# Gate projections first and block products for eight of the conv mixer's projections, in one Trainium2 kernel of a hybrid decoder trunk

## The chip, the cores and the metric

One Trainium2 chip, and one of its cores: the kernel uses no other. The metric is the device time of one execution in microseconds (us), lower is better. The kernel before was run three times: 1012.56, 1013.74 and 1014.99 us, median 1013.74.

## The reference

The reference is a trunk of two layers on 512 tokens of 1024 features, all in float32. The change touches only the first layer's mixer, a short gated convolution:

```
def short_conv_mixer(h, w_in, conv_w, w_out):
    bcx = h @ w_in
    b_gate, c_gate, u = jnp.split(bcx, 3, axis=-1)
    y = b_gate * causal_depthwise_conv3(c_gate * u, conv_w)
    return y @ w_out
...
mix = short_conv_mixer(rmsnorm(h, a_pre_norm[l]), a_w_in[l], a_conv_w[l], a_w_out[l])
h = h + rmsnorm(mix, a_post_norm[l])
```

The three taps run along the tokens. After the mixer come a SwiGLU block (FFN) of layer 0, a layer of sliding-window attention, and the FFN of layer 1; all norms are RMS norms with a gain.

## The kernel before, in words

**Numbers.** Every float32 product is made of three matmuls on rounded halves: each operand is split into a high part (a rounding copy on ACT) and a low part (a subtraction on DVE). `mm3` writes the three matmuls, lines 205 to 207. So each weight tile of 128 x 1024 costs one ACT copy (L490, whi) and one DVE subtraction (L491, wlo) before PE can use it.

**The conv mixer.** The 1024 features are eight tiles of 128, numbered f = 0 to 7. For each tile there are three projections, c, u and b, each a job of 24 matmuls of 128x512 on one weight tile (`conv_jobs`, `project`). PE works on the raw x times the norm gain; the row of reciprocal norms, one number for each token, is multiplied in when DVE takes a job's result from its PSUM bank: `first` takes c (L767), `second` takes u (L770), after which GpSimd (POOL) multiplies the two (L771), `taps` are one TENSOR_SCALAR and two SCALAR_TENSOR_TENSOR on DVE (L774, L777), `third` takes b on DVE (L783) and multiplies on POOL (L784, giving y). For f = 7 the multiplications are on DVE.

**The output projection.** The first four y go in pairs through seven block products P1 to P7 (`seven`, Strassen's scheme, with sums of the blocks of y made by `pair_sums`, L602 to L612); their results are collected in the mix tiles, first by ACT copies (L658), then by DVE adds or subtractions (L660). The last four y are split (`yhi` L788 on ACT, `ylo` L789 on DVE) and used with the weight tiles w0 to w3 in the closing products, whose matmuls write the banks named pmix. The fourth contraction step of the closing's first token tile needs y of f = 7.

**The order.** The opening stage (token halves, tiles f = 0 and 1, norm row) is written out by hand. Then the string `CONV` lists the jobs, and `in_line` runs it: it writes the matmuls of job j, then prepares the weights of job j + 3 (`LINE_LEAD`), then takes steps from the list `late`, into which the jobs put their DVE, ACT and POOL steps. All of this is inside a manual schedule, so each engine executes its instructions in the written order and waits at the first that is not ready. Weights arrive through a queue of SyncE (SP) into seven tiles (`N_RAW`); four split weights (`N_W`) can be held at once. POOL also issues the DMAs that add up blocks of later weights in DRAM (`hsum`, L559), started by `sum_on` at named jobs.

**PSUM.** Eight banks: four in `ps_mm`, two in `ps_sc`, two in `ps_pt`. A bank is handed out in turn within its pool, and the new user waits for the last reader of the old one. P1, P6, P7, P4 collect in two `ps_mm` banks (px), P5 and P3 in the two `ps_sc` banks (pz), P2 in the two `ps_pt` banks (py). The job b6 has its bank in `ps_sc` as well (the string "mms" for f = 6 in the list of pools).

Of the kernel before, what the change touches and what calls it, by code (L numbers as in the profile page):

```python
# [13 lines left out]
ALU = mybir.AluOpType  # L14
# [23 lines left out]
    "c2 u2 b2 c3 u3 b3 c4 u4 b4 c5 u5 P1 P5 b5 P6 P3 c6 P7 P2 u6 P4 b6 w0 c7 u7 w1 b7 w2 w3"  # L38
)

# [41 lines left out]
def yoco_kernel(  # L82
# [8 lines left out]
    w_in: bass.AP,  # L91
    w_ob: bass.AP,
# [134 lines left out]
    xt = [halves("xt") for _ in range(KT // 2)]  # L227
    xt = [xt[k // 2][k % 2] for k in range(KT)]
# [217 lines left out]
    class Raw:  # L446


        def __init__(self, *srcs):
            self.srcs = srcs  # L450
            self.widths = [s.shape[0] * S if len(s.shape) == 3 else D for s in srcs]
            self.n = sum(self.widths)

        def fetch(self):
            self.tile, c = wraw.tile([P, D], F32, tag="raw", name=name("raw")), 0
            for src, n in zip(self.srcs, self.widths):
                dst = self.tile[:, c : c + n]
                if len(src.shape) == 3:
                    src, dst = (src.rearrange("k p c -> p k c"),
                                dst.rearrange("p (k c) -> p k c", c=S))  # L460
                nc.sync.dma_start(dst, src)
                c += n

    class Job:
# [10 lines left out]
        def add(self):  # L475
            if self.make:
                raw = self.raws[0].tile
                nc.vector.tensor_tensor(out=raw, in0=raw, in1=self.raws[1].tile, op=ALU.add)  # L478
# [16 lines left out]
    def in_line(jobs, late, paced=True):  # L495
# [9 lines left out]
        def prepare(j):  # L505

            if 0 <= j < len(jobs):
                jobs[j].prepare()
            while n[0] < len(raws) and (n[0] < N_RAW or raws[n[0] - N_RAW].last <= j):
                raws[n[0]].fetch()  # L510
                n[0] += 1
            if j + 1 < len(jobs):
                jobs[j + 1].add()
# [4 lines left out]
        for j, job in enumerate(jobs):  # L518
# [5 lines left out]
            for _ in range(1 if paced else max(len(late) - 1, 1)):  # L524
                if late and not job.alone:
                    late.pop(0)()
# [141 lines left out]
    rows = slot("rrow")  # L668
# [6 lines left out]
    sums = small.tile([P, 4], F32, tag="sums", name=name("sums"))  # L675
    squares = wide("squares")

    def square(b):
        nc.scalar.activation(squares, hs[b], AF.Square, scale=1 / 32,
                             accum_out=sums[:, b : b + 1])  # L680

    with tc.manual_schedule(engines=ALL):

        warm = small.tile([P, 1], F32, tag="warm", name=name("warm"))
        nc.scalar.activation(warm, ones[:, 0:1], AF.Copy)
        idle = bank("idle", ps_pt)
        for _ in range(WARM):
            nc.tensor.matmul(idle[:, :P], ones, ones, start=True, stop=True)

        def first_hi(i, c0, c1):  # L690
            nc.scalar.activation(ws[i][0][:, c0:c1], first[i][:, c0:c1], AF.Copy)

        def first_lo(i, c0, c1):
            nc.vector.tensor_tensor(out=ws[i][1][:, c0:c1], in0=first[i][:, c0:c1],
                                    in1=ws[i][0][:, c0:c1].bitcast(F32), op=ALU.subtract)

        def token_hi(k):
            nc.scalar.activation(xs[k][0], xt[k], AF.Copy, scale=g(G_APRE, k))

        def token_lo(k):  # L700
            nc.vector.scalar_tensor_tensor(
                out=xs[k][1], in0=xt[k], scalar=g(G_APRE, k), in1=xs[k][0].bitcast(F32),
                op0=ALU.mult, op1=ALU.subtract,
            )

        FIRST = {0: [(0, 0, P), (0, P, 384)], 1: [(0, 384, 768)], 2: [(0, 768, D), (1, 0, S)],
                 4: [(1, S, D)], 5: [(2, 0, S)], 6: [(2, S, D)]}
        for k in range(KT):
            pieces = FIRST.get(k, [])
            token_hi(k)  # L710
            for p in pieces:
                first_hi(*p)
            for p in pieces:
                first_lo(*p)
            token_lo(k)
            for i in range(3):
                for t in range(3):
                    n = 3 * k + t
                    whi, wlo = (w[:, n % KT * P : (n % KT + 1) * P] for w in ws[n // KT])
                    nc.tensor.matmul(begun[0][t], (whi, wlo, whi)[i], xs[k][i == 2],  # L720
                                     start=k == i == 0, stop=k == KT - 1 and i == 2)
        later += [fetch(w_in[1, t]) for t in range(len(later), 3)]
        for b in range(NB):
            hs[b] = wide("h")
            nc.sync.dma_start(hs[b], x[b])
        nc.sync.dma_start(mask, tables[:, 2 * S :])
        nc.sync.dma_start(snk, sinks.partition_broadcast(P))
        ws = [split_weights(None, raw, True) for raw in later[:2]]
        square(0)
        square(1)  # L730
        ws.append(split_weights(None, later[2], True))
        square(2)
        square(3)
        project(begun[1][0], ws[0], xs)
        v = small.tile([P, 4], F32, tag="v", name=name("v"))
        nc.vector.tensor_scalar(out=v, in0=sums, scalar1=EPS, scalar2=None, op0=ALU.add)
        nc.gpsimd.tensor_tensor(out=cols, in0=v, in1=mhalf, op=ALU.pow)
        project(begun[1][1], ws[1], xs)
        pr = bank("pr", ps_pt)
        dg, dhi, dlo = slot("dg"), slot("dhi", F32R), slot("dlo", F32R)  # L740
        for b in range(NB):
            nc.vector.tensor_scalar(out=dg[:, b * P : (b + 1) * P], in0=ident,
                                    scalar1=cols[:, b : b + 1], scalar2=None, op0=ALU.mult)
        nc.scalar.activation(dhi, dg, AF.Copy)
        nc.vector.tensor_tensor(out=dlo, in0=dg, in1=dhi.bitcast(F32), op=ALU.subtract)
        nc.tensor.matmul(pr, ones_r, dlo, start=True, stop=False)
        nc.tensor.matmul(pr, ones_r, dhi, start=False, stop=True)
        nc.scalar.activation(rows, pr, AF.Copy)
        nc.vector.tensor_scalar(out=nsnk, in0=snk, scalar1=-1.0, scalar2=None, op0=ALU.mult)
# [5 lines left out]
    def conv(f, pc=None, pu=None, pb=None):  # L755

        eng = nc.gpsimd if f < KT - 1 else nc.vector
        cr, ur = halves("cru")
        cu, t = halves("cut")
        br, y = halves("bry")  # L760
# [11 lines left out]

        def taps():
# [8 lines left out]
        def third(pb):  # L782
            nc.vector.tensor_tensor(out=br, in0=pb, in1=rows, op=ALU.mult)  # L783
            eng.tensor_tensor(out=y, in0=t, in1=br, op=ALU.mult)  # L784
# [14 lines left out]

        return first, second, taps, third, end  # L800

    def conv_jobs(f, pools):
# [10 lines left out]
        def then(i):  # L813
            def steps():
                first, second, taps, third, end = steps_of
                if i < 2:
# [3 lines left out]
                    if f == KT - 1:  # L820
                        taps()
                        return []
                    return [taps]
# [12 lines left out]
    with tc.manual_schedule(engines=ALL):  # L836
        project(begun[1][2], ws[2], xs)

        def late():
            parts = []  # L840
            for f in range(2):
                first, second, taps, third, end = conv(f)
                first(begun[f][0])
                second(begun[f][1])
                parts += [taps, lambda third=third, f=f: third(begun[f][2])]
                sum_on(f"c{f}")
                issue(len(issues))
            return parts + end()


        product = seven(acts, 2, mix_c, True)
        b11, b12, b22, b21 = (Raw(w_ob[b]) for b in range(4))
        line = {
            f"P{p}": Job(raws, lambda job, p=p: product(p, range(2), *job.w), None, len(raws) > 1)
            for p, *raws in ((1, b11), (5, b11, b12), (6, b11, b22), (3, b22), (7, b12, b22),
                             (2, b21), (4, b11, b21))
        }
        pools = {"p": ps_pt, "m": ps_mm, "s": ps_sc}
        for f, of in zip(range(2, KT), ("ppm", "mmm", "ssp", "mmp", "mms", "spm")):
            for c, job in zip("cub", conv_jobs(f, [pools[p] for p in of])):  # L860
                line[f"{c}{f}"] = job
        for n in range(4):
            line[f"w{n}"] = closing = Job([Raw(w_out[n // 2, n % 2])], None)
            closing.slots = True
        in_line([line[n] for n in CONV.split()], late, False)
        ws = [line[f"w{n}"].w for n in range(4)]
# [787 lines left out]
def _lay_out(x, a_pre_norm, a_w_in, a_conv_w, a_w_out, a_post_norm, ffn_pre_norm,  # L1654
# [39 lines left out]
    for b in (0, HD):  # L1694
# [9 lines left out]
    wi = c(wi[[1, 2, 0]].transpose(1, 0, 2, 3))  # L1704
    wi[0] = wi[0].reshape(3, P, KT, P).transpose(2, 0, 1, 3).reshape(3, KT, P, P).transpose(
# [13 lines left out]
        "w_in": wi,  # L1719
        "w_ob": c(blocks(np.asarray(a_w_out[0])[: D // 2])),  # L1720
# [26 lines left out]
```

## Time and profile before

| what | value |
|---|---|
| median of 3 runs | 1013.74 us (1012.56 to 1014.99) |
| the profiled execution | 1012.5 us, of which the span of the profile is 1010.7 us |
| POOL busy | 203.9 us, 20% |
| ACT busy | 588.4 us, 58% |
| jobs of the conv line end, first pmix matmul | 155.37 us |

A row of the profile's timeline is: start, duration, engine, line, operation, output<-input, shapes, and in brackets the idle time of that engine ahead of the row and what ended it. A row of its stretches is: from:to, PE busy, busy time of each engine with the number of instructions, the granted clock as a share, the share of the DMA engines, GB/s. In the groups by line, busy time and mean duration come first and idle time ahead of the group's instructions after the second bar.

### The profile page before, as it was taken

What the parts mean: (1) busy time and instruction counts of PE and PEld (TensorE: products, weight loads), DVE (VectorE), ACT (ScalarE), POOL (GpSimd) and SP (SyncE); (2) the same over time, 40 slices, a digit from 0 to 9 for tenths busy, and PEclk for the clock granted to TensorE, in tenths of its full rate; (3) what the DMA queues carried; (4) which work ended last, traced back from release to release, by engine and by line L of the source; (5) the groups of instructions that cost most, each with busy time, mean ns of one, the idle gap of its engine ahead of it and who ended that gap; (6) DMA issues with size and microseconds to landing.
All of it is one profiled execution on the core that took longest, in us unless ns stands there. A gap on an engine that the chain in (4) does not pass through costs nothing.

```text
span 1010.7 us, 16083 instructions
## 1 busy us (share of the span) xinstructions
PE 1002.3 (99%) x5864; PEld 882.4 (87%) x5864; DVE 887.7 (88%) x1525; ACT 588.4 (58%) x1061; POOL 203.9 (20%) x264
## 2 busy tenths in 40 slices
PE   9999999999999999999999999999999999999997
PEld 8888888999889898898898888789998888989986
DVE  5766767899789999999888998888997999999996
ACT  6322444875656465566385788777666564645641
POOL 0443033102101011000022657321211010110001
PEclk9999999999999999999999999999999999999999
DMA  9997789649979789779603889966999577979742
GB/s 357 293 252 241 180 248 334 185 167 268 334 246 288 250 287 311 240 214 343 209 1 120 225 236 245 303 233 176 295 288 330 167 247 235 284 277 266 247 174 84
DMA packets 66575, 244.50 MB, mean 242 GB/s; under 512 B 7872, under 2 KB 8384, under 8 KB 54720
## 3 DMA queue, kind: packets, MB, share of 16 engines
q1 hardware_dynamic: 51328, 145.98, 38.8%
q0 software_dynamic: 14592, 96.48, 37.6%
q10 hardware_dynamic: 576, 1.02, 0.3%
q8 instruction: 46, 0.75, 0.3%
q14 instruction: 33, 0.27, 0.1%
HBM read 237.15 MB, written 102.76 MB: 336 GB/s over the span
## 4 chain that ended last, share of the span: by engine, by line
PE 97%; DVE 2%; ACT 1%; issue 0%; DVEq 0%
PE gx L1093 15%; PE gx L1096 8%; PE pcub L207 4%; PE pcub L205 4%; PE pcub L206 4%; PE px L206 4%; PE px L205 4%; PE px L207 4%; PE pmix L207 3%; PE pmix L205 3%; PE pmix L206 3%; PE gz L1093 3%; PE gy L206 2%; PE gy L205 2%; PE gy L207 2%; PE pz L206 2%
## 5 line engine op out<-in xcount | busy, mean ns | idle before, releaser
L491 DVE TENSOR_TENSOR wlo<-raw,whi 128x1024 fp32r<-128x1024 f32 x225 | 274.6, 1225 | 33.8 <-ACT whi L490 33.7
L490 ACT ACTIVATE whi<-raw 128x1024 fp32r<-128x1024 f32 x225 | 233.7, 1051 | 99.1 <-DVE raw L478 28.7
L1093 PE MATMUL gx<-xt,whi 128*128 128x512 f32 x480 | 120.7, 393 | 0.0
L1093 PEld LDWEIGHTS gx<-xt,whi 128*128 128x128 f32 x480 | 86.2, 189 | 15.7
L559 POOL DMA_DIRECT2D hsum<-in_w_gb_dram x96 | 64.4, 757 | 135.0 <-ACT whi L490 89.6
L559 POOL DMA_DIRECT2D hsum<-hsum x32 | 25.3, 792 | 304.8 <-ACT whi L490 219.7
L1048 DVE TENSOR_TENSOR st<-gx,st 128x256 f32<-128x256 f32 x200 | 77.5, 419 | 2.2 <-ACT st L1071 0.4
L1071 ACT ACTIVATE st<-gx 128x256 f32<-128x256 f32 x120 | 43.5, 380 | 60.9 <-PE gx L1096 57.2
L1096 PEld LDWEIGHTS gx<-xt,wlo 128*128 128x128 f32 x480 | 65.5, 190 | 4.7
L1096 PE MATMUL gx<-xt,wlo 128*128 128x256 f32 x480 | 66.9, 282 | 0.0
L1107 ACT ACTIVATE gr<-gr 128x1024 f32<-128x1024 f32 x20 | 21.2, 1062 | 55.6 <-DVE gr L1048 55.6
L205 PE MATMUL px<-wlo,ahi 128*128 128x512 f32 x120 | 46.7, 389 | 0.0
L206 PE MATMUL px<-whi,ahi 128*128 128x512 f32 x120 | 46.7, 389 | 0.0
L207 PE MATMUL px<-whi,alo 128*128 128x512 f32 x120 | 46.7, 389 | 0.0
L205 PE MATMUL gy<-xlo,whi 128*128 128x256 f32 x160 | 45.3, 283 | 0.0
L206 PE MATMUL gy<-xhi,whi 128*128 128x256 f32 x160 | 45.3, 283 | 0.0
L207 PE MATMUL gy<-xhi,wlo 128*128 128x256 f32 x160 | 45.3, 283 | 0.0
L559 POOL DMA_DIRECT2D hsum<-in_w_dn_dram x48 | 32.6, 794 | 47.3 <-ACT whi L490 47.3
L1093 PE MATMUL gx<-xhl,whi 128*128 128x512 f32 x160 | 39.9, 391 | 0.0
L312 POOL TENSOR_TENSOR ur<-uv,mhalf 128x1 f32<-128x1 f32 x15 | 13.9, 929 | 119.8 <-DVE uv L308 119.8
L660 DVE TENSOR_TENSOR mix<-mix,px 128x512 f32<-128x512 f32 x54 | 34.8, 682 | 2.2 <-PE px L207 2.2
L478 DVE TENSOR_TENSOR raw<-raw,raw 128x1024 f32<-128x1024 f32 x28 | 34.1, 1219 | 0.0
(322 smaller groups left out, 2996.8 us busy)
## 6 DMA issues: line engine op xcount, KB each, us to landing
hsum<-in_w_gb_dram POOLq DMA_DIRECT2D x96, 512.0 KB, 8.0
raw<-hsum SPq DMA_DIRECT2D x88, 512.0 KB, 7.9
raw<-in_w_gb_dram SPq DMA_DIRECT2D x60, 512.0 KB, 7.0
hsum<-in_w_dn_dram POOLq DMA_DIRECT2D x36, 512.0 KB, 8.2
raw<-in_w_dn_dram SPq DMA_DIRECT2D x32, 512.0 KB, 6.2
hsum<-hsum POOLq DMA_DIRECT2D x28, 512.0 KB, 5.7
raw<-in_w_in_dram SPq DMA_DIRECT2D x21, 512.0 KB, 7.4
hsum<-in_w_dn_dram POOLq DMA_DIRECT2D x12, 768.0 KB, 12.1
```

Source lines behind the costliest of these rows:

```text
L205: nc.tensor.matmul(out, whi, xlo, start=start, stop=False, **kw)
L206: nc.tensor.matmul(out, whi, xhi, start=False, stop=False, **kw)
L207: nc.tensor.matmul(out, wlo, xhi, start=False, stop=stop, **kw)
L478: nc.vector.tensor_tensor(out=raw, in0=raw, in1=self.raws[1].tile, op=ALU.add)
L490: self.begun = nc.scalar.activation(hi[:, :n], raw, AF.Copy)
L491: nc.vector.tensor_tensor(out=lo[:, :n], in0=raw, in1=hi[:, :n].bitcast(F32), op=ALU.subtract)
L559: nc.gpsimd.dma_start(dst, src, max_dma_last_dim=4 * 4 * S, **kw))
L660: nc.vector.tensor_tensor(out=m, in0=m, in1=banks[bs][r], op=ALU.subtract if half else ALU.add)
L1048: nc.vector.tensor_tensor(out=out, in0=a, in1=b, op=ALU.add)
L1071: nc.scalar.activation(ste, a, AF.Copy)
L1093: nc.tensor.matmul(banks[c][e], whi[:, kk], factors[p][k][2], start=opened and k == 0, stop=False, **kw)
L1096: nc.tensor.matmul(banks[c][e][:, :256], wlo[:, kk], factors[p][k][0], start=False, stop=k == 3 and p in (4, 5), **kw)
```

## The change

The string of jobs, which sets the order of everything in this stage:

```
 CONV = (
-    "c2 u2 b2 c3 u3 b3 c4 u4 b4 c5 u5 P1 P5 b5 P6 P3 c6 P7 P2 u6 P4 b6 w0 c7 u7 w1 b7 w2 w3"
+    "b2 b3 b4 b5 X1 X2 X6 X5 X7 X3 X4 Y1 Y2 Y6 Y5 Y7 Y3 Y4 c6 P1 P5 u6 P6 P3 b6 P7 P2 c7 P4 w0 u7 w1 b7 w2 w3"
 )
```

The eight jobs c2, u2 to c5, u5 are replaced by fourteen block products. X1 to X7 give c and u of tiles 2 and 3, Y1 to Y7 those of tiles 4 and 5. Each is 24 matmuls of 128x256. The block sums of x are made once in the opening: 4 scaled copies, 16 sums of 128x256 (`combine`, DVE) and 8 high and 8 low parts of 512 elements. The block sums of the weights are made for each pair by four DVE additions of 128x1024 (`make_two`, `make_three`, `make_four`, all at L907). The results are collected by `take`:

```
+        chain = {1: "X", 6: "X", 7: "X", 4: "X", 5: "Z", 3: "Z", 2: "Y"}
+        pools = {"X": ps_mm, "Y": ps_pt, "Z": ps_sc}
...
+            if p in (1, 6):
+                nc.scalar.activation(st, x, AF.Copy)
+            elif p == 5:
+                nc.scalar.activation(u, z, AF.Copy)
+            elif p == 2:
+                nc.vector.tensor_tensor(out=g0, in0=tiles(y), in1=tiles(st), op=ALU.add)
+            elif p == 3:
+                nc.vector.tensor_tensor(out=g1, in0=tiles(z), in1=tiles(st), op=ALU.add)
+            elif p == 7:
+                nc.vector.tensor_tensor(out=u, in0=x, in1=u, op=ALU.add)
+            else:
+                for gg, m in ((g0, x), (g1, u)):
+                    nc.vector.scalar_tensor_tensor(out=gg, in0=tiles(m), scalar=-1.0, in1=gg,
+                                                   op0=ALU.mult, op1=ALU.mult)
```

So for f = 2 to 5 the product c times u is formed on DVE within `take`, POOL's multiplication at the old L771 is gone there, and the norm row enters afterwards as its square:

```
+        def square_rows():
+            nc.vector.tensor_tensor(out=cu, in0=cu, in1=rows2, op=ALU.mult)
```

The jobs b2 to b5 (`gate_job`) run first and leave b times the norm row in a tile each until the taps are done. The steps of tiles 0 and 1 (their taps, gates and pair sums) are taken two behind each of the first four jobs, then one behind each. The norm's squares are now taken over eight half tiles `own`, overwritten in place; x itself is loaded a second time, as h, when u6's steps are written:

```
+                    for b in range(NB):
+                        hs[b] = wide("h")
+                        tc.keep_in_program_order(nc.sync.dma_start(hs[b], x[b]))
                     return [taps]
```

The weight sums in DRAM start at other jobs (c2's at b3, c3's at X2, c4's at Y1, c5's at Y7). From P1 on the line stands in another order, and c6, u6, b6 keep their pools. Three places show what that does to the engines' order. The first is PE at the end of P3 (banks pz), before: behind P3 follows c6, with a bank of `ps_mm`.

```order
L205 MATMUL pz_257_1023<-wlo_261_1041,ahi_232_877 128x512
L206 MATMUL pz_257_1023<-whi_260_1040,ahi_232_877 128x512
L207 MATMUL pz_257_1023<-whi_260_1040,alo_233_878 128x512
L205 MATMUL pcub_274_1121<-xhl_99_220,whi_263_1069 128x512
L206 MATMUL pcub_274_1121<-xhl_99_220,whi_263_1069 128x512
```

Now the same place, where behind P3 follows b6, whose bank (pcub_312) is the one that pz_291 held:

```order
L210 MATMUL pz_291_1323<-whi_295_1341,alo_274_1253 128x512
L208 MATMUL pz_292_1324<-wlo_296_1342,ahi_273_1252 128x512
L209 MATMUL pz_292_1324<-whi_295_1341,ahi_273_1252 128x512
L210 MATMUL pz_292_1324<-whi_295_1341,alo_274_1253 128x512
L208 MATMUL pcub_312_1434<-xhl_99_220,whi_298_1373 128x512
L209 MATMUL pcub_312_1434<-xhl_99_220,whi_298_1373 128x512
```

So the first matmul of b6 stands behind DVE's reading of pz_291. The second place is that reading on DVE, which in the kernel now stands at the end of this piece (taps of f = 5, L848 and L851; weight parts, L498; the sum for P7, L485; u6's take, L841; the low part of y of f = 4, L864; the takes of P3, L667):

```order
L848 TENSOR_SCALAR t_278_1261<-gr_247_1002,gt_84 128x512
L851 SCALAR_TENSOR_TENSOR t_278_1261<-gr_247_1002,gt_84,t_278_1261 128x511
L851 SCALAR_TENSOR_TENSOR t_278_1261<-gr_247_1002,gt_84,t_278_1261 128x510
L498 TENSOR_TENSOR wlo_299_1374<-raw_259_1110,whi_298_1373 128x1024
L485 TENSOR_TENSOR raw_256_1104<-raw_256_1104,raw_258_1108 128x1024
L841 TENSOR_TENSOR cru_279_1262<-pcub_297_1348,rrow_111_232 128x512
L498 TENSOR_TENSOR wlo_305_1405<-raw_256_1104,whi_304_1404 128x1024
L864 TENSOR_TENSOR ylo_307_1409<-bry_201_711,yhi_306_1408 128x512
L667 TENSOR_TENSOR mix_287_1312<-mix_287_1312,pz_291_1323 128x512
L667 TENSOR_TENSOR mix_288_1314<-mix_288_1314,pz_292_1324 128x512
```

Before, the same takes stand here (L660), behind weight parts of c6 and P7 and the take of b5, with no job of PE right behind that uses their banks:

```order
L491 TENSOR_TENSOR wlo_264_1070<-raw_215_788,whi_263_1069 128x1024
L478 TENSOR_TENSOR raw_200_681<-raw_200_681,raw_211_755 128x1024
L491 TENSOR_TENSOR wlo_266_1091<-raw_200_681,whi_265_1090 128x1024
L783 TENSOR_TENSOR bry_241_928<-pcub_262_1044,rrow_111_232 128x512
L660 TENSOR_TENSOR mix_252_1011<-mix_252_1011,pz_256_1022 128x512
L660 TENSOR_TENSOR mix_253_1013<-mix_253_1013,pz_257_1023 128x512
```

What moved: the taps of f = 4 and 5, the last block-product takes and the row squares now stand a few rows ahead of the takes of P3, and b6 stands behind them on PE. The third place is the end of the line on DVE, from the taps of f = 7 to the low part of its y. Before, the fourth gate-up weight part (the second L437) stands behind the take of b7 (L783):

```order
L195 TENSOR_TENSOR wlo_322_1384<-raw_290_1204,whi_320_1382 128x512
L195 TENSOR_TENSOR wlo_323_1385<-raw_290_1204,whi_321_1383 128x512
L783 TENSOR_TENSOR bry_309_1310<-pcub_324_1390,rrow_111_232 128x512
L437 TENSOR_TENSOR wlo_341_1472<-raw_336_1454,whi_340_1471 128x1024
L784 TENSOR_TENSOR bry_309_1310<-cut_308_1309,bry_309_1310 128x512
L789 TENSOR_TENSOR ylo_326_1421<-bry_309_1310,yhi_325_1420 128x512
```

Now it stands ahead of that take (L858), between the two halves of w3's low part:

```order
L198 TENSOR_TENSOR wlo_352_1632<-raw_322_1498,whi_350_1630 128x512
L440 TENSOR_TENSOR wlo_371_1720<-raw_366_1702,whi_370_1719 128x1024
L198 TENSOR_TENSOR wlo_353_1633<-raw_322_1498,whi_351_1631 128x512
L858 TENSOR_TENSOR bry_333_1532<-pcub_354_1638,rrow_111_232 128x512
L859 TENSOR_TENSOR bry_333_1532<-cut_332_1531,bry_333_1532 128x512
L864 TENSOR_TENSOR ylo_356_1669<-bry_333_1532,yhi_355_1668 128x512
```

What moved: the take of b7 has one more weight part, with its ACT copy, ahead of it. And the job P4, whose result ACT copies into the mix tiles, stands behind c7 instead of ahead of b6, so ACT's splits of w1, b7, w2 and the gate-up weights come behind a product that ends two jobs later in the line.

More of the change, by code (lines that the diff above doesn't have):

```diff
@@ L509, in prepare @@
             while n[0] < len(raws) and (n[0] < N_RAW or raws[n[0] - N_RAW].last <= j):
[L510 removed]
+                raws[n[0]].fetch(not paced and n[0] < 4)
                 n[0] += 1
@@ L673, in yoco_kernel @@
              for f in range(2)]
-    sums = small.tile([P, 4], F32, tag="sums", name=name("sums"))
-    squares = wide("squares")
+    sums = small.tile([P, 8], F32, tag="sums", name=name("sums"))
+    own = [[slot("own") for _ in range(2)] for _ in range(NB)]
     def square(b):
[L679 to L749, printed above, removed]
@@ L834, in conv_jobs @@
         return [Job([Raw(w_in[f, i])], run(i), then(i)) for i in range(3)]
[L836 to L866, printed above, removed]
@@ new lines, in late @@
+    def late():
+        parts = []
+        for f in range(2):
+            first, second, taps, third, end = opened[f]
+            parts += [taps, lambda third=third, f=f: third(begun[f][2])]
+            sum_on(f"c{f}")
+            issue(len(issues))
+        return parts + end()
+    product = seven(acts, 2, mix_c, True)
+    b11, b12, b22, b21 = (Raw(w_ob[b]) for b in range(4))
+    line = {
+        f"P{p}": Job(raws, lambda job, p=p: product(p, range(2), *job.w), None, len(raws) > 1)
+        for p, *raws in ((1, b11), (5, b11, b12), (6, b11, b22), (3, b22), (7, b12, b22),
+                         (2, b21), (4, b11, b21))
+    }
@@ L869, in tile_done @@
+    in_line([line[n] for n in CONV.split()], late, False)
+    ws = [line[f"w{n}"].w for n in range(4)]
+    opening.close()
     def tile_done(res, t, square=True):
```

243 lines of the change are left out of this document (230 added, 13 removed).

## The prediction

> **What bounds the kernel now.** The page comes first: the engines' shares and the chain that ended last.
>
> ```profile
> span 1010.7 us, 16083 instructions
> PE 1002.3 (99%) x5864; PEld 882.4 (87%) x5864; DVE 887.7 (88%) x1525; ACT 588.4 (58%) x1061; POOL 203.9 (20%) x264
> ...
> PE 97%; DVE 2%; ACT 1%; issue 0%; DVEq 0%
> ```
>
> PE is busy for 99% and makes up 97% of the chain: only fewer or shorter matmuls shorten the kernel, and every new wait of PE lengthens it. DVE, at 88%, is next. What it has to spare in the stage that changes is in the table of stretches (columns: PE, PEld, DVE, ACT, POOL busy).
>
> ```profile
> 0.00:25.00 25.00, 23.94 (x106) 20.35 (x107) 13.61 (x25) 17.35 (x31) 0.70 (x6) 1.00 0.95 356
> 25.00:50.00 25.00, 25.00 (x112) 20.67 (x111) 19.26 (x30) 7.95 (x12) 11.46 (x13) 1.00 0.91 295
> 50.00:75.00 25.00, 25.00 (x112) 20.71 (x111) 17.17 (x21) 6.53 (x8) 9.86 (x10) 1.00 0.94 247
> 75.00:100.00 25.00, 25.00 (x112) 20.71 (x111) 17.37 (x22) 6.34 (x8) 7.58 (x10) 1.00 0.79 241
> 100.00:125.00 25.00, 25.00 (x112) 20.67 (x112) 16.94 (x20) 13.00 (x17) 3.46 (x4) 1.00 0.72 192
> ```
>
> From 25 us on PE has no gap, the granted clock is 1.00, and DVE is busy for only some 17 of 25 us: eight spare. The change spends from that store. The last view is the timeline, for cadences:
>
> ```profile
> 24.31 0.39 PE L205 MATMUL pcub<-xlo,whi 128*128 128x512 f32 x1
> 27.03 0.39 PE L205 MATMUL pcub<-xhl,whi 128*128 128x512 f32 x1
> ...
> 181.77 0.28 PE L205 MATMUL pgu<-xhl,whi 128*128 128x256 f32 x1
> 187.41 0.28 PE L207 MATMUL pgu<-xhi,wlo 128*128 128x256 f32 x1
> ```
>
> The first two lie 12 matmuls apart: 2.72 / 12 = 0.2267 us for 512 columns. The last two lie 47 apart: 5.64 / 47 = 0.120 us for 256. That is 0.0067 more than half.
>
> **Term 1, PE's work.** Removed: 8 jobs x 24 x 0.2267 = 43.5 us. Added: 14 products x 24 x 0.120 = 40.3 us. Gain 3.2 us, and no more than that anywhere, since P1 to P7, c6 to b7 and the closing keep their matmuls. The row says 256 columns cost a little over half. [...]
>
> **Term 2, what DVE must do before b6.** The place is the end of P3: b6's bank is the one that DVE's take of pz still has to empty, so PE waits if DVE is late. The prices, from start to start:
>
> ```profile
> 75.92 0.42 DVE L606 SCALAR_TENSOR_TENSOR s<-s,yy 128x256 f32<-128x256 f32 x1
> 76.26 0.42 DVE L605 TENSOR_TENSOR s<-yy 128x256 f32<-128x256 f32 x1
> ...
> 93.93 1.23 DVE L491 TENSOR_TENSOR wlo<-raw,whi 128x1024 fp32r<-128x1024 f32 x1 [0.23 <-ACT whi L490]
> 95.07 1.22 DVE L478 TENSOR_TENSOR raw<-raw,raw 128x1024 f32<-128x1024 f32 x1
> ...
> 103.89 0.48 DVE L774 TENSOR_SCALAR cut<-cut,gt 128x512 f32<-128x512 f32 x1
> 104.41 1.54 DVE L777 SCALAR_TENSOR_TENSOR cut<-cut,gt 128x511 f32<-128x511 f32 x2
> 105.86 2.35 DVE L491 TENSOR_TENSOR wlo<-raw,whi 128x1024 fp32r<-128x1024 f32 x2
> ...
> 115.37 1.28 DVE L660 TENSOR_TENSOR mix<-mix,pz 128x512 f32<-128x512 f32 x2
> 116.56 1.41 DVE L491 TENSOR_TENSOR wlo<-raw,whi 128x1024 fp32r<-128x1024 f32 x1
> ```
>
> So a 1024-wide operation takes 1.14, a 512-wide TENSOR_TENSOR 0.60 (1.19 for two), a SCALAR_TENSOR_TENSOR 0.73 (1.45 for two), a TENSOR_SCALAR 0.52, a 256-wide one 0.35. Between the end of b2 and the take of P3, DVE's new order holds 34 of 1024 (23 weight parts, 8 block sums at L907, 3 sums for P5, P6, P7), 25 TENSOR_TENSOR of 512 (among them 4 row squares and the takes of the blocks), 16 SCALAR_TENSOR_TENSOR (12 taps, 4 products in the takes), 6 TENSOR_SCALAR and 10 of 256: 38.8 + 15.0 + 11.7 + 3.1 + 3.5 = 72.1 us. PE does b3, b4, b5 (3 x 5.44), 14 x 2.88, c6, P1 P5, u6, P6 P3 (4 x 5.44) in the same time: 78.4 us. Only 6.3 us are spare.
>
> Two things eat them. First, waiting for ACT's whi or for a load: the row at 93.93 shows 0.23 us ahead of a weight part, 23 times 5.3 at most, 0 at least; I take 4, since a DVE that is behind finds whi ready. Second, POOL. Seven of its 512-wide multiplications fall in the stretch (four y of the pairs, y of f = 4 and 5, c times u of f = 6), and this is what one does to DVE:
>
> ```profile
> 66.64 1.29 POOL L771 TENSOR_TENSOR cut<-cru 128x512 f32<-128x512 f32 x1 [5.79 <-DVE cru L770]
> ...
> 115.60 1.29 POOL L784 TENSOR_TENSOR bry<-cut,bry 128x512 f32<-128x512 f32 x1 [13.42 <-DVE bry L783]
> ```
>
> ```profile
> 66.67 2.34 DVE L491 TENSOR_TENSOR wlo<-raw,whi 128x1024 fp32r<-128x1024 f32 x1 [0.17 <-ACT whi L490]
> ```
>
> The weight part at 66.67 took 2.34 instead of 1.23, ending one such part after POOL: 1.11 us lost. The takes at 115.37 read PSUM and lost nothing. Seven hits are 7.8 us, none is 0. PSUM reads and TENSOR_SCALAR make up about 11.5 of the 72 us, so 84% of hits tell, and the two of tiles 0 and 1 come early enough to be absorbed by later waits for weights: 5 x 0.84 x 1.11 = 4.7. DVE then arrives 72.1 + 4 + 4.7 = 80.8 us after b2, against 78.4. The bank's last matmul lies three matmuls ahead of P3's end and the take lasts 0.69: if DVE is on time b6 waits about 0.3 us; here 80.8 - 78.4 + 0.75 = **3.2 us**. With all hits and 4 us of waiting it is 83.9 - 78.4 + 0.75 = 6.3. Behind b6's wait stands everything on PE, so it counts in full.
>
> [...]
>
> **Term 3, the products themselves.** X4 and Y4 accumulate in the bank that DVE reads for product 7, with one product (2.88 us) between. With DVE on time that hides the 0.60. In Y, DVE has just done the taps of f = 2 and POOL its y: a POOL hit of 1.11 may show. Between 0 and 1.1, I take **0.5**.
>
> **Term 4, the opening.** DVE gets 16 sums of 256 and 8 low parts of 512 more, 16 x 0.35 + 8 x 0.60 = 10.4 us, of which four low parts stand ahead of b2's weights; in the first two stretches it has 11.4 + 5.7 us idle. Between 0 and one low part, 0.6; I take **0.2**. The second load of x (2 MB) has nobody waiting until the closing, over 20 us after its issue at u6, so it is costed at nothing; if it delays the gate-up weights, that lies in term 5.
>
> **Term 5, the end of the line.** Before, the last y is just in time:
>
> ```profile
> 133.13 1.28 ACT L658 ACTIVATE mix<-px 128x512 f32<-128x512 f32 x2 [8.05 <-PE px L207]
> ...
> 155.34 1.06 ACT L432 ACTIVATE whi<-raw 128x1024 fp32r<-128x1024 f32 x1 [3.86 <-PE pcub L206]
> 158.29 0.63 ACT L788 ACTIVATE yhi<-bry 128x512 fp32r<-128x512 f32 x1 [1.89 <-DVE bry L784]
> ```
>
> ```profile
> 155.81 0.69 DVE L783 TENSOR_TENSOR bry<-pcub,rrow 128x512 f32<-128x512 f32 x1
> 156.43 1.23 DVE L437 TENSOR_TENSOR wlo<-raw,whi 128x1024 fp32r<-128x1024 f32 x1
> 157.58 0.68 DVE L784 TENSOR_TENSOR bry<-cut,bry 128x512 f32<-128x512 f32 x1
> 158.96 0.69 DVE L789 TENSOR_TENSOR ylo<-bry,yhi 128x512 fp32r<-128x512 f32 x1 [0.70 <-ACT yhi L788]
> ```
>
> ```profile
> 155.37 0.39 PE L205 MATMUL pmix<-wlo,yhi 128*128 128x512 f32 x1
> ...
> 159.45 0.39 PE L205 MATMUL pmix<-wlo,yhi 128*128 128x512 f32 x1
> 159.67 0.39 PE L206 MATMUL pmix<-whi,yhi 128*128 128x512 f32 x1
> 159.90 0.39 PE L207 MATMUL pmix<-whi,ylo 128*128 128x512 f32 x1
> ```
>
> The closing starts at 155.37 and asks for y of f = 7 after 18 matmuls, at 159.45, and for its low part at 159.90; yhi ends at 158.92, ylo at 159.65. In the new order the gate-up part, which cannot start before its whi (155.34 + 1.06), stands ahead of the take of b7. Then: weight part 156.43, half of w3 157.57, take 158.17, y 158.77, yhi 159.5 to 160.1, ylo to 160.85. That is 0.7 late, and 0.95 with the low part: about 1.0 even if all else is early. ACT is not early. It stands at the copies of P4 (the row at 133.13 waited for PE in the same way), and now only u7 and b7 follow on PE: 10.88 + 4.08 = 14.96 us. From P4's end come copies and the first split of w1 (1.28 + 0.57), then on DVE 5 of 1024, 10 of 512 and one set of taps: 5.7 + 6.0 + 1.97, then yhi, 0.7: 16.2 us, so 1.2 late, 1.5 with the low part. If gate-up weights land late behind the second load of x, up to 3.0; I take **1.8**, between 1.0 and 3.0.
>
> **Sum.** -3.2 + 3.2 + 0.5 + 0.2 + 1.8 = +2.5 us. After the closing nothing changes, so it carries through: the profiled run of 1012.5 (span 1010.7) would become 1015.0, and the median, which lies 1.2 above the profiled run, 1013.74 + 2.5 = 1016.2 us. All low ends give -3.2 + 0.3 + 0 + 0 + 1.0 = -1.9, all high ends -3.2 + 6.3 + 1.1 + 0.6 + 3.0 = +7.8. A difference of 0.2%, 2.0 us, is about what a measurement of this kernel can tell.
>
> **The rivals.**
>
> 1. *DVE keeps ahead, so it is not slower.* It decides at P3: if DVE starts the take of pz within 1 us of the last matmul. For it: 6.3 us are spare on paper, and POOL's early multiplications can fall on waits. Against: eight block sums and 20 extra takes and squares come without a pause. -3.2 + 0.3 + 0.2 + 1.0 = -1.7: 1012.0. Chance 0.21.
> 2. *The last y is in time as well, so it is faster.* ACT and DVE would have to reach b7's take with nothing ahead of it, as if the gate-up part were done earlier. -3.2 + 0.3 + 0.2 = -2.7: 1011.0. Against it stands the order itself. Chance 0.14.
> 3. *POOL and DVE shut each other out every time.* By the row at 66.67 all seven hits tell and none is absorbed; b6 waits 6.3, product 4 of Y 1.1, the end 2.2: -3.2 + 6.3 + 1.1 + 0.2 + 2.2 = +6.6: 1020.3. For it: DVE has an operation ready at nearly every moment. [...] Chance 0.20.
> 4. *The change does not do what it says:* the products run late on weights (four blocks are needed for X2 and its sum), and PE's gain of 3.2 goes into gaps. 2.5 + 3.2 = +5.7: 1019.4. Against: seven raw tiles and three jobs of lead. Chance 0.05.
>
> **How the numbers follow.** The forecast has 0.40, with its own range 1013.5 to 1018.5. A quarter of it is within 2 us: same gets 0.10 + 0.20 of rival 1 = 0.30; faster 0.14 of rival 2 + 0.01 of rival 1 = 0.15; slower 0.30 + 0.20 + 0.05 = 0.55. The range 1011.3 to 1020.5 leaves out half of rivals 2 and a third of rival 3.
>
> **What would show it.** In the profile after: PE's span of the fourteen products 40.3 us; one gap of PE at b6 whose releaser is DVE's mix<-mix,pz, about 3 us; a second gap in the closing's first pmix matmuls, released by yhi, 1 to 2 us; DVE busy over 23 of 25 us from 50 to 125. It is wrong if b6 starts without a gap, if the gap lies at a load, or if the products' matmuls are not 0.120 us apart.

## The result, and the profile after

The changed kernel took 1025.09 us (median of 4 runs, 1024.37 to 1025.84), the kernel before, measured beside it, 1013.29: ratio 1.0114, 95% interval 1.0097 to 1.0132, so 11.8 us slower. The direction was forecast, the size was not: +2.5 us were predicted, and the range ended at 1020.5.

The page of the changed kernel, in the lines that answer to those of before:

```profile
span 1023.2 us, 16452 instructions
PE 1005.2 (98%) x6008; PEld 890.1 (87%) x6008; DVE 921.8 (90%) x1569; ACT 603.6 (59%) x1094; POOL 201.7 (20%) x260
...
PE 89%; DVE 6%; DMA 3%; ACT 1%; issue 1%; DVEq 0%; SPq 0%; ACTq 0%
```

PE's share of the chain fell from 97 to 89%: DVE has 6%, and DMA, which had none, 3%. The view of waits of PE says where (waited for, total us, times, longest):

```profile
PE pcub L208 <- DVE mix L667: 4.6, 1, 4.6
PE pmix L208 <- ACT yhi L863: 2.8, 1, 2.8
PE pmix L208 <- DVE wlo L198: 1.7, 1, 1.7
...
PE gx L208 <- DVE st L939: 0.5, 1, 0.5
```

These are the places of the prediction: b6 behind P3, the last y in the closing, Y4 behind the take of Y7. A second wait of the closing, on the weight half that stands ahead of the last y, is new. The table of stretches shows what was not foreseen at all (the last three columns are the granted clock, the DMA share and GB/s):

```profile
75.00:100.00 25.00, 24.48 (x204) 24.30 (x203) 24.13 (x27) 10.43 (x13) 7.61 (x8) 1.00 0.97 312
100.00:125.00 25.00, 24.11 (x116) 20.00 (x114) 24.69 (x31) 10.63 (x15) 5.51 (x5) 1.00 0.58 146
125.00:150.00 25.00, 21.32 (x85) 17.45 (x86) 17.69 (x22) 7.58 (x11) 7.77 (x10) 0.86 0.97 311
150.00:175.00 25.00, 20.50 (x81) 16.14 (x80) 17.34 (x24) 10.94 (x18) 0.33 (x1) 0.86 0.87 300
```

DVE is full from 75 to 125 us (24.1 and 24.7 of 25, 17 before), as forecast. But the granted clock, 1.00 before, is 0.86 in both stretches that hold a long wait. PE's timeline at b6:

```profile
123.72 0.39 PE L210 MATMUL pz<-whi,alo 128*128 128x512 f32 x1
128.68 0.77 PE L208 MATMUL pcub<-xhl,whi 128*128 128x512 f32 x1 [4.57 <-DVE mix L667]
...
130.09 0.63 PE L208 MATMUL pcub<-xhl,whi 128*128 128x512 f32 x1
130.52 0.63 PE L209 MATMUL pcub<-xhl,whi 128*128 128x512 f32 x1
...
133.60 0.40 PE L208 MATMUL pcub<-xlo,whi 128*128 128x512 f32 x1
...
164.01 0.39 PE L210 MATMUL pmix<-whi,ylo 128*128 128x512 f32 x1
166.14 0.50 PE L208 MATMUL pmix<-wlo,yhi 128*128 128x512 f32 x1 [1.74 <-DVE wlo L198]
...
166.72 0.39 PE L210 MATMUL pmix<-whi,ylo 128*128 128x512 f32 x1
169.87 0.79 PE L208 MATMUL pmix<-wlo,yhi 128*128 128x512 f32 x1 [2.76 <-ACT yhi L863]
...
174.47 0.39 PE L210 MATMUL pmix<-whi,ylo 128*128 128x512 f32 x1
```

The gap at b6 is 128.68 - 123.72 - 0.23 = 4.73 us. Then the matmuls come 0.43 us apart (130.09, 130.52), with 0.50 of the clock granted, up to 133.60: twelve steps in 4.92 us instead of 2.72, another 2.20. In the closing the gaps are 1.90 and 2.92, and the slow steps after the second cost 2.11 (169.87 to 174.47, eleven steps, against 2.49), those between the two 0.13.

The sum by terms, start to start: -3.2 (PE's work), +0.93 (the opening: the norm row's matmul starts at 33.40 instead of 32.47), +0.68 (Y4), +4.73 (b6), +4.82 (the closing's two gaps), +4.44 (slow matmuls) = +12.4. The first matmul of the next stage, which turns the normed tiles, starts at 188.33 instead of 175.77, 12.56 later, and the span is 12.5 longer: everything lies in this stage.

Why the closing waits for so long shows on ACT, at the splits of the gate-up weights:

```profile
161.20 1.06 ACT L435 ACTIVATE whi<-raw 128x1024 fp32r<-128x1024 f32 x1 [3.75 <-DMA raw<-in_w_gu_dram]
```

ACT stands at a gate-up weight that has not landed (3.75 us, and 0.92 at the next one), and the halves of w3 and the last y stand behind it. From the DMA view of 125 to 170 us, these loads in the kernel before and in the changed one (count, KB each, median us to landing):

```profile
raw<-in_w_gu_dram SPq DMA_DIRECT2D x4, 512.0 KB, 5.6
```

```profile
raw<-in_w_gu_dram SPq DMA_DIRECT2D x4, 512.0 KB, 11.5
```

They are issued 12.4 us later (from 141.13 on, 128.70 before) and take twice as long. Whose traffic they meet was open at this point.

### The profile page after: what moved, and what is told of

Its sections match the earlier page's. It is cut to its first block, busy times and chain, and to the rows that moved or that the text cites. A ratio compares the mean times of both kernels' runs of the same rounds, so it can differ in the third digit from the quotient of the medians.

```text
span 1023.2 us, 16452 instructions
## 1 busy us (share of the span) xinstructions
PE 1005.2 (98%) x6008; PEld 890.1 (87%) x6008; DVE 921.8 (90%) x1569; ACT 603.6 (59%) x1094; POOL 201.7 (20%) x260
## 4 chain that ended last, share of the span: by engine, by line
PE 89%; DVE 6%; DMA 3%; ACT 1%; issue 1%; DVEq 0%; SPq 0%; ACTq 0%
PE gx L1282 14%; PE gx L1285 7%; PE px L208 3%; PE px L209 3%; PE px L210 3%; PE pmix L208 3%; PE pmix L210 3%; PE pmix L209 3%; PE gz L1282 3%; PE gy L209 2%; PE gy L208 2%; PE gy L210 2%; PE pcub L774 2%; DVE wlo L498 2%; PE pz L208 2%; PE pz L210 2%
## 5 line engine op out<-in xcount | busy, mean ns | idle before, releaser
L498 DVE TENSOR_TENSOR wlo<-raw,whi 128x1024 fp32r<-128x1024 f32 (+1 forms) x231 | 283.9, 1233 | 18.9 <-ACT whi L497 18.8
L497 ACT ACTIVATE whi<-raw 128x1024 fp32r<-128x1024 f32 (+1 forms) x231 | 239.6, 1051 | 97.8 <-DVE raw L485 31.8
L208 PE MATMUL gy<-xlo,whi 128*128 128x256 f32 x176 | 49.8, 283 | 0.0
L209 PE MATMUL gy<-xhi,whi 128*128 128x256 f32 x176 | 49.8, 283 | 0.0
L210 PE MATMUL gy<-xhi,wlo 128*128 128x256 f32 x176 | 49.8, 283 | 0.0
L667 DVE TENSOR_TENSOR mix<-mix,px 128x512 f32<-128x512 f32 x54 | 35.0, 684 | 5.6 <-PE px L210 5.6
L485 DVE TENSOR_TENSOR raw<-raw,raw 128x1024 f32<-128x1024 f32 x28 | 35.2, 1259 | 0.0
```

The lines of the kernel that those rows point to most:

```text
L208: nc.tensor.matmul(out, whi, xlo, start=start, stop=False, **kw)
L209: nc.tensor.matmul(out, whi, xhi, start=False, stop=False, **kw)
L210: nc.tensor.matmul(out, wlo, xhi, start=False, stop=stop, **kw)
L497: self.begun = nc.scalar.activation(hi[:, :n], raw, AF.Copy)
L498: nc.vector.tensor_tensor(out=lo[:, :n], in0=raw, in1=hi[:, :n].bitcast(F32), op=ALU.subtract)
L667: nc.vector.tensor_tensor(out=m, in0=m, in1=banks[bs][r], op=ALU.subtract if half else ALU.add)
```

## The experiments

**Theory A**: each wait of PE is a loss of its own, and a long one also drops the clock; the waits come from the order on DVE and ACT. **Theory B**: the end of the line is set by the landing of the gate-up weights, so PE's earlier gains are given back there. **Theory C**, after the first four runs: those weights land late since they meet the sums in DRAM that POOL issues late.

**e1: b6 in another pool.**

```
-    for f, of in zip(range(CROSS[1], KT), ("mms", "spm")):
+    for f, of in zip(range(CROSS[1], KT), ("mmm", "spm")):
```

> One edit to the changed kernel (1025.1 us): the bank of b6 comes from ps_mm, so b6 no longer waits for DVE's take of P3. Theory A (the wait at b6, 4.7 us, and the slow matmuls behind it, 11 at 0.427 instead of 0.227 us, 2.2 us, are a loss of their own): both go, 1025.1 - 6.9 = 1018.2 us, within 1.5, no granted clock under 0.95 from 125 to 150 us, and the gaps in the closing as before. Theory B (the end of the line is set by when the gate-up weights land, not by PE): PE reaches the closing 6.9 us earlier and waits there for most of that, 1022 to 1025 us, with gaps in pmix of 8 us or more.

Measured: 1023.46 us (1.0103 of before, 1.0087 to 1.0118). The wait at b6 and its slow clock are gone, but of 6.9 us only 1.6 came out:

```profile
PE pmix L208 <- DVE wlo L198: 7.9, 1, 7.9
PE pmix L208 <- ACT yhi L863: 2.1, 1, 2.1
```

The closing now waits 10 us. So theory B holds for the end of the line, and b6's wait, though real, was mostly not what set the time. The gate-up loads start 4.2 us earlier (136.90), but take 16.5 us.

**e2: POOL's multiplications on DVE.**

```
-        eng = nc.gpsimd if f < KT - 1 else nc.vector
+        eng = nc.vector
```

> One edit to the changed kernel: the multiplications that POOL did (y, and c times u of f = 6) are done by DVE, 0.60 us each. Theory A (POOL shuts DVE out: in the trace the seven multiplications lengthened DVE's operations by 6.2 us): 7 x 0.60 = 4.2 us replace 6.2, the wait at b6 falls from 4.7 to about 2.7 us, the slow matmuls behind it go too if the clock falls only after longer waits: 1025.1 - 2.0 - 2.2 = 1020.9 us, between 1020 and 1023. Rival (DVE is simply overloaded, POOL's work is beside it): DVE gets 4.2 us more, the wait at b6 grows to about 9 us: 1029 us.

Measured: 1017.97 us (1.0046, 1.0029 to 1.0063), 7.1 us faster than the changed kernel, more than forecast.

```profile
PE pcub L208 <- DVE mix L667: 2.6, 1, 2.6
PE gx L208 <- DVE st L939: 2.1, 1, 2.1
PE pmix L208 <- ACT yhi L863: 1.1, 1, 1.1
```

The wait at b6 is 2.6 us, near the 2.7 worked out, but partly by luck. Between its takes of b2 and P3, DVE is busy for 76.4 us (44.65 to 128.75) in place of 78.3 (44.98 to 127.86) in the changed kernel, though it has seven operations more: POOL's own had cost it more than 0.60 us each, as theory A says. Yet DVE reaches the take of P3 0.9 us later, not 2.0 earlier, since it stood at a load on the way:

```profile
80.63 1.23 DVE L907 TENSOR_TENSOR raw<-raw,raw 128x1024 f32<-128x1024 f32 x1 [3.44 <-DMA raw<-in_w_cu_dram]
```

b6 waits for less because PE comes to it 2.9 us later, after waits of 2.1, 0.9 and 0.3 us in the products, where the changed kernel has 0.5. The 2.6 us were still followed by slow matmuls (0.63 granted from 128 to 132 us). The surprise is the closing, which waits 1.1 us instead of 4.5. The DMA view of the same stretch:

```profile
raw<-in_w_gu_dram SPq DMA_DIRECT2D x4, 512.0 KB, 3.9
```

The gate-up weights, issued at the same time as in the changed kernel (141.25), land in 3.9 us, and no sum is among the transfers of that stretch. The changed kernel's POOL timeline shows where its sums stand:

```profile
93.31 2.16 POOL L859 TENSOR_TENSOR yy<-t,bry 128x512 f32<-128x512 f32 x1 [14.56 <-issue]
97.41 2.19 POOL L859 TENSOR_TENSOR yy<-t,bry 128x512 f32<-128x512 f32 x1 [1.94 <-DVE t L851]
...
116.94 2.14 POOL L859 TENSOR_TENSOR bry<-t,bry 128x512 f32<-128x512 f32 x1 [15.72 <-DVE t L851]
...
126.19 0.79 POOL L566 DMA_DIRECT2D hsum<-hsum  x1
126.73 1.30 POOL L566 DMA_DIRECT2D hsum<-in_w_gb_dram  x2
141.85 1.30 POOL L859 TENSOR_TENSOR bry<-cut,bry 128x512 f32<-128x512 f32 x1 [13.83 <-DVE bry L858]
143.10 0.84 POOL L566 DMA_DIRECT2D hsum<-hsum  x1
143.66 2.94 POOL L566 DMA_DIRECT2D hsum<-in_w_gb_dram  x4
```

POOL's rows come in the written order. Three DMAs of sums stand behind the multiplications that waited 15.72, 2.01 and 1.76 us for DVE (the first is shown), five more behind the y of f = 6, which waited 13.83 us; the eight go out at 126 to 147 us, after a spell with the DMA engines idle (share 0.00 from 115 to 120 us). In e2 the same eight go out from 88 to 103 us. The kernel before issues its last sums no earlier (133 to 147 us), but its gate-up loads start at 128.70, ahead of most of them. So it is the loads that moved, into the stretch of the sums.

**e3: P4 ahead of c7.**

```
-... u6 P6 P3 b6 P7 P2 c7 P4 w0 u7 w1 b7 w2 w3
+... u6 P6 P3 b6 P7 P2 P4 c7 w0 u7 w1 b7 w2 w3
```

> One edit to the changed kernel: P4 stands ahead of c7 instead of behind it, which also puts the fourth gate-up split behind the take of b7. Theory A (ACT's copies of P4 and DVE's order set the end of the line): the waits in pmix fall from 4.8 us to about 1, the slow matmuls behind them, 2.1 us, go: 1025.1 - 5.9 = 1019.2 us, between 1018 and 1021. Theory B (landing of the gate-up weights sets it): the waits stay within 1 us of 4.8: 1024 to 1025.5 us.

Measured: 1023.70 us (1.0104, 1.0089 to 1.0119), 1.4 us faster than the changed kernel, about the spread of its runs (1022.53 to 1024.79). The waits in pmix are 0.9 and 2.6 us, the gate-up loads still take 12.0 us. ACT is free earlier and waits for them instead (6.1 us). Theory A fails for the closing.

**e4: the second load of x 11 us earlier** (the four DMAs written at c6's step instead of u6's).

> One edit to the changed kernel: the second load of x is written at c6's step instead of u6's, some 11 us earlier, where the DMA engines idle (share 0.00 from 115 to 120 us). Theory B (the gate-up weights land late behind that load): they land about 5 us earlier, ACT no longer waits 3.8 and 0.9 us for them, waits in pmix fall from 4.8 to 1 to 2 us and the slow matmuls go: 1019 to 1021.5 us. Theory A (ACT's copies of P4 and the order): no change beyond 1 us, 1024 to 1025.5 us.

Measured: 1024.25 us (1.0107, 1.0092 to 1.0122), 0.8 us faster, less than the spread of its runs (1023.01 to 1024.44). The waits in pmix are 2.3 and 2.5 us.

```profile
raw<-in_w_gu_dram SPq DMA_DIRECT2D x4, 512.0 KB, 11.8
```

The load of x is issued from 110.33 on, clear of the gate-up weights, and they land as late as before: it is not what they wait behind.

**e5 and e6: the price of one wait, in the kernel before.** Between c3 and u3, with 4 and with 9 copies:

```
+                if f == 3 and i == 1:
+                    z = slot("z", F32R)
+                    for _ in range(4):
+                        nc.scalar.activation(z, pss[0], AF.Copy)
+                    nc.tensor.matmul(pss[1][:, :P], z[:, :P], z[:, :P], start=True, stop=True)
                 project(pss[i], job.w, xs)
```

> The kernel before, with one wait of PE between c3 and u3 and nothing else: ACT copies c3's bank 4 times into a scratch tile, and a 128x128 matmul on that tile opens u3's bank. 4 copies at 0.52 and the way there and back: a gap of about 2.4 us. Theory (the granted clock falls only after a wait longer than about 2.9 us, the longest in the changed kernel and its variants so far that no slow matmul followed being 2.6): the matmuls behind it keep 0.227 us, 1013.2 + 2.4 = 1015.6 us. Rival (any wait drops the clock): 1017.8 us.

> The same with 9 copies: a gap of about 5.0 us. Theory: about 10 matmuls behind it run at 0.427 us instead of 0.227, 2.1 us more: 1013.2 + 5.0 + 2.1 = 1020.3 us. Rival (the slow matmuls of the changed kernel come from something else, such as its narrower matmuls): 1018.2 us and no slow matmul.

Measured: 1018.68 us (1.0055, 1.0039 to 1.0072) and 1022.09 us (1.0091, 1.0076 to 1.0106), so 5.8 and 9.2 us for gaps that came out longer than meant, 3.3 and 6.4 us of idle time, since the copies began behind DVE's take of c3. PE with 4 copies:

```profile
60.67 0.39 PE L207 MATMUL pcub<-xhi,wlo 128*128 128x512 f32 x1
64.36 0.33 PE L814 MATMUL pcub<-z 128*128 128x128 f32 x1 [3.30 <-ACT z L813]
...
65.24 0.63 PE L207 MATMUL pcub<-xhl,wlo 128*128 128x512 f32 x1
65.67 0.63 PE L205 MATMUL pcub<-xhl,whi 128*128 128x512 f32 x1
```

The slow steps of 0.43 us are there in the kernel before, with 512 columns and none of the change's products, so the drop belongs to the wait. Both are cases of a long wait. With 4 copies the gap is 64.36 - 60.67 - 0.23 = 3.46 us, the extra matmul takes 0.16, and the slow steps add 1.7 us (step by step against 0.227); the rest of the 5.8 us stands ahead of all this, in the opening of that profile (0.74 us). With 9 copies the gap is 6.60 us and the slow steps add 2.8. The short case was not made here. The expectation's statement that no slow matmul had followed a wait of 2.6 us was a misreading of e2.

**e7: the late sums behind the closing.**

```
-                sum_on(f"c{f}")
-                issue(len(issues))
                 parts = [lambda: third(pss[2])] + end()
...
-    sum_on("o0")
-    issue(len(issues))
...
+            for at in ("c6", "c7", "o0", "o1"):
+                sum_on(at)
+                issue(len(issues))
```

> The changed kernel, with the DRAM sums of weights that POOL issued from c6's jobs to the closing (nine DMAs between 126 and 147 us) issued behind the closing instead. Theory C (the gate-up weights land late since their loads, which now start 12 us later, meet those sums): they land about 5 us earlier, the waits in pmix fall from 4.8 to 1 to 2 us and the slow matmuls behind them go, 1025.1 - 3.3 - 2.1 = 1019.7 us, unless a later sum is missed in the FFN. Rival (P4's place and DVE's order alone set the end of the line): 1024 to 1025.5 us.

Measured: 1041.43 us (1.0282, 1.0267 to 1.0298), slower, by a new wait behind the closing: POOL's reciprocal root for the next token tile now stands behind those DMAs.

```profile
PE xt L353 <- ACT xn L342: 20.9, 2, 16.9
PE pcub L208 <- DVE mix L667: 4.6, 1, 4.6
PE pmix L208 <- ACT yhi L863: 1.1, 1, 1.1
```

Up to the closing it answers the question: b6 waits as in the changed kernel, but the closing 1.1 instead of 4.5 us, and the loads are fast:

```profile
raw<-in_w_gu_dram SPq DMA_DIRECT2D x4, 512.0 KB, 4.1
```

Theory C holds: without the sums' traffic the gate-up loads, issued from 140.05 on, so nearly as late as in the changed kernel, take 4.1 us instead of 11.5.

**e8 and e9: the edits of e2 and e1 together, then with e3's too.**

> Both edits: DVE does the multiplications of POOL, and b6 has its bank in ps_mm. From e2 (1018.0 us): the 2.6 us wait at b6 goes, 1015.4 us if nothing takes its place (theory A), 1017 to 1018 us if the closing then waits for its last y by as much (theory B); not under 1013.5, since the waits for the products' weights and product 4 (3.3 us in e2) stay.

> Three edits to the changed kernel: DVE does POOL's multiplications, b6 has its bank in ps_mm, P4 stands ahead of c7. From e8 (1017.4 us, one wait in pmix of 1.6 us, the last y behind the fourth gate-up split): with that split behind the take of b7 the wait falls to about 0.5, 1016.3 us (1015.5 to 1017). If the sums and loads set the end after all: 1017.4.

Measured: e8 1017.43 us (1.0039, 1.0026 to 1.0052), e9 1016.03 us (1.0025, 1.0015 to 1.0035). In e8 the 2.6 us at b6 are gone, yet only 0.5 is gained: the wait for the last y rose from 1.1 to 1.6, and slow matmuls followed the 2.1 us at Y4 in e8's profile, though not in e2's. In e9 the wait for the last y falls to 0.7 (0.5 expected):

```profile
PE gx L208 <- DVE st L939: 2.1, 1, 2.1
...
PE pmix L208 <- ACT yhi L863: 0.7, 1, 0.7
```

**e10: tiles 2 and 3 alone by block products**, with the rest of the line in its old order.

```
+    "b2 b3 X1 X2 X6 X5 X7 X3 X4 c4 u4 b4 c5 u5 P1 P5 b5 P6 P3 c6 P7 P2 u6 P4 b6 w0 c7 u7 w1 b7 w2 w3"
...
+CROSS = (2, 4)
```

> Only tiles 2 and 3 by block products (b2 b3 first, X1 to X7), tiles 4 and 5 and the rest of the line as in the kernel before, x loaded again at u6's step. PE saves half of 3.2 us, 1.6; the opening costs 0.9 as in the changed kernel; DVE has four row squares, four block sums and four takes fewer, and the places of P3, b6 and P4 are as before, so that no long wait is left there. Theory A: 1013.0 - 1.6 + 0.9 = 1012.3 us, and the end of the line costs up to 1 us from the second load of x: 1012 to 1013.5, no difference from the kernel before that can be measured. Theory B (the second load of x alone makes the gate-up weights late): waits in pmix of 3 us or more and a slower clock behind them, 1017 us.

Measured: 1019.69 us (1.0071, 1.0057 to 1.0084). Both theories miss. The closing waits only 1.2 us; the loss is a wait of X6 for ACT's copy of X1, with a slow clock behind it (0.50 from 60 to 64 us):

```profile
PE gx L208 <- ACT st L931: 4.7, 1, 4.7
```

With b4 and b5 no longer ahead of X1, that copy (60.06 on ACT) stands right behind ACT's splits of the pair sums of tiles 0 and 1, which wait for POOL's y (14.41 us, up to 53.17). In the changed kernel the four gate jobs at the head of the line would hide that; no run tests it alone. The closing's wait is short although the gate-up loads take 10.6 us beside the sums: the first of them starts at 134.72, 6.4 us earlier than in the changed kernel.

**e11: e9 with c6 between Y3 and Y4.**

```
-... Y1 Y2 Y6 Y5 Y7 Y3 Y4 c6 P1 ...
+... Y1 Y2 Y6 Y5 Y7 Y3 c6 Y4 P1 ...
```

> The kernel of e9 (1016.0 us) with c6 between Y3 and Y4, so that Y4 no longer waits for DVE's take of Y7. In e9 that wait was 2.1 us, and the 16 matmuls of 256 columns behind it ran at 0.213 instead of 0.120 us, 1.5 us. Theory A (each wait and its slow matmuls are losses of their own once the closing is in time): 1016.0 - 3.6 = 1012.4 us, no difference from the kernel before that can be measured. Theory B (the end of the line takes it back, DVE being the bound): the wait in pmix grows from 0.7 to 2 us or more, 1014 to 1016 us.

Measured: 1016.71 us (1.0038, 1.0026 to 1.0050). The wait of Y4 is gone, others have come:

```profile
PE pmix L208 <- ACT yhi L863: 1.6, 1, 1.6
PE px L208 <- DVE mix L667: 1.1, 1, 1.1
```

The first of them was followed by slow matmuls (0.74 granted from 164 to 168 us). So what PE gains earlier comes back as waits on DVE and at the last y. That is theory B's pattern, with DVE in the place of the loads, though not its numbers: the wait in pmix grew to 1.6 us, not to 2 or more, and the time lies above its range. Six runs lie between 1013.7 and 1017.9. No version tried was faster than the kernel before.

## Why the prediction was wrong

**Term 1, PE's work: right.** The matmuls of 256 columns are 0.120 us apart where nothing waits (the stretch from 50 to 75 us is without a gap), so the 3.2 us are there.

**Term 2, DVE ahead of b6: right in mechanism, low in size.** 3.2 us forecast, 4.73 measured, 6.3 the stated end. The sum of 72.1 us held: from the take of b2 to that of P3 DVE needs 82.9 us, of which POOL takes 6.2 and waits 3.9 (4 were allowed), which leaves 72.8. POOL cost more than the 4.7 us. Its multiplications lengthened seven DVE operations by 6.2 us in all. From DVE's timeline of the changed kernel:

```profile
117.85 1.52 DVE L848 TENSOR_SCALAR t<-gr,gt 128x512 f32<-128x512 f32 x1
...
121.99 2.31 DVE L485 TENSOR_TENSOR raw<-raw,raw 128x1024 f32<-128x1024 f32 x1
...
125.47 1.86 DVE L498 TENSOR_TENSOR wlo<-raw,whi 128x1024 fp32r<-128x1024 f32 x1 [0.57 <-ACT whi L497]
```

The 84% in that term, and so the 4.7, counts PSUM reads and TENSOR_SCALAR as spared. The takes at 115.37 in the kernel before show the first (1.28 us for two beside a multiplication); no run shows the second: here TENSOR_SCALAR took 1.52 instead of 0.48. e2 shows what POOL cost by its sign: with the same multiplications on DVE itself, DVE is busy for 1.9 us less up to the take of P3. But e1 showed that this term, although it is there, was worth only 1.6 us of the time as long as the closing waited.

**The step that failed first: pricing a wait at its own length.** "Behind b6's wait stands everything on PE, so it counts in full" stops short. A long wait also costs the clock: 4.4 us in the changed kernel, over a third of the loss, and nothing in the terms allowed for it. It is the largest part of the 9.9 us between the forecast +2.5 and the +12.4 of the sum by terms; the closing has 3.0 of them, b6 1.5, the opening 0.7, Y4 0.2. The trace of before could not show it, having no long wait of PE; e5 and e6 put one there and got the same drop. Length alone does not decide: the same wait of 2.1 us at Y4 was followed by slow matmuls, 0.213 instead of 0.120 us apart, in e8 and e9, but not in e2.

The records of the granted clock settle which waits are enough. In the changed kernel and in all of e1 to e11 the clock, until the last 20 us of the kernel, falls to 0.50 for 3.41 us or for two, three or six times that, and the falls within one profile lie whole multiples of 3.41 us apart (126.37 and 167.33 in the changed kernel, 12 x 3.413). With each profile cut into stretches of 3.413 us at these points, what decides is how much of a wait falls into one of them. Here is Y4's wait, 2.1 us in both kernels, first in e2, then in e9:

```profile
98.34:101.75 3.41, 1.66 (x14) 1.45 (x13) 3.41 (x5) 0.98 (x2) 1.96 (x5) 1.00 1.05 396
101.75:105.17 3.42, 3.08 (x25) 3.12 (x26) 3.39 (x7) 1.01 (x2) 0.73 (x2) 1.00 1.09 266
```

```profile
99.07:102.48 3.41, 1.34 (x12) 1.17 (x11) 3.41 (x6) 1.36 (x2) 2.21 (x4) 1.00 1.08 350
102.48:105.89 3.41, 3.41 (x17) 3.41 (x18) 3.38 (x6) 0.63 (x1) 0.00 (x0) 0.50 1.01 240
```

In e2 the cut divides the wait, and the clock stays at 1.00; in e9 all of it lies in one stretch (PE busy 1.34 of 3.41 us instead of 1.66), and the next one runs at 0.50. Counting a matmul as 0.227 us at 512 columns, 0.120 at 256 and, as an estimate, half of that, 0.06, at 128, every stretch at full clock behind which the clock fell held at most 1.31 us of matmuls, and every one behind which it stayed held at least 1.32 (all thirteen profiles, from 20 us to 1000 us). The two groups lie close, but do not overlap. So about 2.1 us of waiting within one stretch is the limit in these profiles.

**The step that failed second: term 5**, "if gate-up weights land late behind the second load of x, up to 3.0; I take 1.8". The two gaps were 4.82 us. The second load of x was the wrong cause (e4). The weights were issued 12.4 us late and so met the sums in DRAM, which in both kernels stand on POOL behind multiplications that wait for DVE (e2 and e7). The prediction counted POOL's seven multiplications as a cost to DVE and did not ask what stood behind them on POOL's own queue, nor which loads would move into its way. By the prediction's own sign, a gap that lies at a load, this part is wrong: the closing's wait goes back to one. P4's place, which the prediction took for the cause, is worth about 1.4 us (e3 against the changed kernel, e9 against e8), hardly more than the spread of the runs.

**Term 3** was 0.68 against 0.5. **Term 4** was 0.93 against 0.2, outside its bounds (0 to 0.6): the low part of the norm row's diagonal is later on DVE than one 512-wide part explains. No run took that apart.

**The rivals.** Rival 3 (POOL and DVE shut each other out every time) came nearest, with b6 4.73 against 6.3 and Y4 0.68 against 1.1, and would still have been 5 us short, for the clock and the sums. Rivals 1, 2 and 4 did not happen.

What stays open: why DVE's opening part is 0.9 us late, and why the gate-up loads are issued 12.4 us later. They start earlier where b6 does not wait (136.90 in e1), so they follow PE in part, but no run took the rest apart.

## What to carry to other kernels

A saving of a few microseconds on the busiest engine is worth nothing if it fills the next engine: here 3.2 us of matmuls were bought with a DVE that had 6.3 of 78 us spare, and each order tried gave back more. Price a new wait of PE of some 2 us or more with the slow matmuls behind it (1.4 to 2.8 us here), and ask of every in-order engine that comes to wait what else stands in its queue; on POOL it was DMAs, and urgent loads had moved into the stretch in which they came out. When one of several waits is removed and little is gained, look for a later wait that has grown by as much before doubting the first.

## What the runs showed of the hardware that was not expected

- After a long wait of PE the matmuls run at half the clock, 0.427 us for 512 columns and 0.213 for 256 (e9, behind Y4), for some 3 to 5.6 us, which costs 1.4 us (e2, behind b6) to 2.8 us (e6). Waits of 2.6 us and more (2.6 in e2; 2.8, 4.6; 3.3, 4.7, 6.4, 7.9) were all followed by it, none of up to 1.2 us by itself was, and between them it happened or not: 1.6 us did in e11 and did not in e8, 2.1 us did in e8 and e9 and did not in e2. What separated them was whether about 2.1 us of waiting, the short pauses beside a wait counted in, fell into one stretch of 3.41 us on the fixed grid of the clock's records.
- Four loads of 512 KB land in 4 to 5 us (3.9 in e2, 4.1 in e7; also e8, e9, e11) without the sums from DRAM to DRAM beside them and in 10.6 to 16.5 with them (11.5 in the changed kernel, 16.5 in e1, 12.0 in e3, 11.8 in e4, 10.6 in e10).
- A TENSOR_SCALAR of 128x512 in float32, with one input tile, was held up by a POOL multiplication as much as operations with two: 1.52 instead of 0.48 us, which it takes in e2, where POOL does none, so 1.04 longer; the sum of two tiles of 128x1024 at 121.99 took 2.31 instead of 1.22, 1.09 longer.
